# A transformer layer on one core: the MLP's down-projection by seven block products over pairs of weight blocks

## The chip, the core and the metric

The kernel runs on one core of a Trainium2 chip. The core has a matrix engine (TensorE, PE in the profile; its loads of the stationary operand are PEld), a vector engine (VectorE, DVE), a scalar engine (ScalarE, ACT), a general engine (GpSimd, POOL) and an engine that issues transfers (SyncE, SP). Each engine works through its own queue in order, and waits on semaphores for the others. Matrix products end in PSUM, eight banks of 128 x 512 float32, which TensorE, VectorE and ScalarE use here and GpSimd does not; everything else is in SBUF or in DRAM. The metric is the device time of one execution in microseconds. The kernel before took 2886.45 us (median of three runs, 2884.72 to 2888.83).

## What is computed

One layer of a hybrid model on 2048 tokens of width 1024: retention and attention, an output projection, a gated residual, and then an MLP whose activation is a squared ReLU. Only the MLP and the last norm are touched by the change:

```python
def _sqrelu_mlp(h, w1, w2):
    return jnp.square(jax.nn.relu(h @ w1)) @ w2

    h2 = _modulate(_rmsnorm(x, norm2_g), sh2, sc2)
    x = x + g2 * _sqrelu_mlp(h2, w_ff1, w_ff2)
...
    return _rmsnorm(x, final_norm_g)
```

`w_ff1` is 1024 x 4096 and `w_ff2` is 4096 x 1024, all in float32.

## The kernel before

The kernel is one program in three overlapping stages; the schedule is written out by hand (`tc.manual_schedule()`), so the order of the code is the order of each engine's queue. Until about 1575 us it does the projections, retention, attention and the output projection; functions are put into numbered steps by `on(k, phase, ...)`, and the last of these steps already holds the beginning of the MLP (`prelude`). From 1606 us on it does nothing but the MLP.

**Precision.** Every float32 operand of a product is split into a high and a low float16 part (`split16`, lines 70 to 72: ScalarE writes the high part, VectorE or GpSimd subtracts it and writes the low part). A product is then three matmuls: high by high, high by low, low by high.

**The up-projection** (`up_part`, lines 1705 to 1714) is done by seven block products in place of eight. The tokens are taken in two halves of 1024 (`halves`); the 4096 columns of `w_ff1` in 16 blocks of 256. For one half and one block the weights are four tiles `a11` to `a22` (halves of the 1024 rows by 128 columns). Sums of them (`s1` to `s4`, `sum_w1`, GpSimd, line 1641) and of the tokens (`h_pair`, made once for each half, stored in DRAM as `hf` and held in SBUF) enter seven products of 4 x 3 matmuls with 512 columns each. Each product has a PSUM bank to itself (`pu`, four banks), and `up_out` adds the seven to running sums in SBUF on VectorE, straight from PSUM (line 1735), once on ScalarE (line 1740). Then come the ReLU (ScalarE, line 1723), the square (GpSimd, `r * r`, line 1724) and the split (ScalarE and VectorE, lines 71 and 72).

**The down-projection** (`down`, lines 1766 to 1775) is an ordinary one. For a half and a block, each of the eight groups of 128 tokens and each of the two halves of the 1024 output columns takes 2 x 3 matmuls into a bank of PSUM (`pd`), and VectorE adds the bank to the accumulator of those tokens in SBUF (line 1775). The rows of `w_ff2` are fetched for each block in each half of the tokens, so twice (`ws`), scaled by the gate on GpSimd (line 1696) and split (lines 71 and 72).

**The order of the work.** The main loop at the end of `layer_kernel` goes over 32 blocks (16 for each half). In a block, all seven up products come first, then the sixteen down groups; small jobs of the other engines are put in between by hand: the sums and splits of the next block's `w_ff1` (`sum_w1`, `form_w1`, lines 1641, 1650 and 1651), the making of `w_ff2` (`make_w2`), the remaining sums of the second half's tokens (`h_pair(1, ...)`), the end of the first half (`ending`: squares, root, scaling, storing, loading the second half's accumulators). `rest` holds the last steps of the last tile of the attention stage (`transpose_x`, `modulate`, `shift_`, `store_h`), which the main loop works off in its first blocks.

## Time and profile before

| what | value |
|---|---|
| median of three runs | 2886.45 us (2884.72 to 2888.83) |
| the profiled execution | 2882.76 us, of which its span 2881.0 us |
| mean granted TensorE clock | 0.990 |
| TensorE busy with matmuls | 2732.5 us, 95% of the span |
| VectorE busy | 2119.7 us, 74% |
| GpSimd busy | 1524.2 us, 53% |
| ScalarE busy | 1430.4 us, 50% |
| matmuls of the up-projection | 3 lines x 896 = 2688 |
| matmuls of the down-projection | 3 lines x 1024 = 3072 |

How to read the lines shown later: a group of instructions is given as line, engine, operation, what it writes and reads, how often, then its busy time in us and the mean of one in ns, and after the second bar the idle time of its engine just ahead of it with what ended that. A matmul's own duration (some 380 ns) is longer than its distance from the next one, since matmuls follow each other in a pipeline; the distance is what counts, and it is read from the number of matmuls in a stretch of time. In a table of windows each engine has its busy time and, in brackets, the number of its instructions.

### The profile page before, as it was taken

Reading aid. Unit: us, or ns where it says so; the run is one execution under the profiler, and the core shown is the slowest. Engines: PE = TensorE matmul, PEld = TensorE weight load, DVE = VectorE, ACT = ScalarE, POOL = GpSimd, SP = SyncE. Lnnn points to the kernel's source line nnn. Section 1 sums busy time; section 2 is a strip of 40 time slices with the busy share of each in tenths; the row PEclk is TensorE's granted clock in tenths of the full one; section 3 lists DMA queues with packets and bytes.
Section 4 is the critical chain, followed back from the end, with each engine's and each line's share of the span. In section 5 each row is a group of like instructions: output and inputs, shape, how many; then the busy total and the mean of one; then the engine's idle time right before and its main releaser. Section 6 shows DMA issues by size and latency. Waiting matters only on the chain. (4 is left out here: it accounts for less than half of the span.)

```text
span 2881.0 us, 45242 instructions
## 1 busy us (share of the span) xinstructions
PE 2732.5 (95%) x17152; PEld 1455.9 (51%) x17152; DVE 2119.7 (74%) x3324; ACT 1430.4 (50%) x2419; POOL 1524.2 (53%) x1289
## 2 busy tenths in 40 slices
PE   7999999988899999999998899999999999999998
PEld 2545644545566666666565344444444444444443
DVE  4856777478878778777875577777777777777776
ACT  3634752237777777777776233342333333333332
POOL 2623762447667568776776465663443434444432
PEclk9999999999999999999999999999999999999999
DMA  7478667562112122332224623231114411111111
GB/s 258 130 254 300 207 203 230 169 196 63 55 62 78 59 69 86 93 98 63 89 80 165 223 81 97 82 97 59 59 59 155 152 59 59 59 48 48 52 44 59
DMA packets 249656, 323.87 MB, mean 112 GB/s; under 512 B 105111, under 2 KB 156311, under 8 KB 247646
## 3 DMA queue, kind: packets, MB, share of 16 engines
q1 hardware_dynamic: 249150, 319.93, 34.4%
q8 instruction: 135, 2.21, 0.3%
q10 hardware_dynamic: 288, 1.05, 0.1%
q14 instruction: 83, 0.68, 0.1%
HBM read 249.45 MB, written 71.46 MB: 111 GB/s over the span
## 5 line engine op out<-in xcount | busy, mean ns | idle before, releaser
L180 DVE TENSOR_REDUCE nm<-mp 128x1 f32<-128x512 f32 (+1 forms) x576 | 389.8, 684 | 155.3 <-PE mp L167 126.6
L221 POOL TENSOR_TENSOR plo<-p,phi 128x1024 f16<-128x1024 f32 x160 | 352.7, 2206 | 164.9 <-ACT phi L214 136.2
L210 ACT ACTIVATE p<-st 128x512 f32<-128x512 f32 x576 | 337.9, 598 | 181.0 <-PE st L205 107.3
L1772 PE MATMUL pd<-w2hi,uhi 128*128 128x512 f16 x1024 | 388.0, 379 | 12.6 <-DVE acc L1775 12.4
L1773 PE MATMUL pd<-w2lo,uhi 128*128 128x512 f16 x1024 | 388.0, 379 | 0.6 <-DVE w2lo L72 0.6
L1774 PE MATMUL pd<-w2hi,ulo 128*128 128x512 f16 x1024 | 388.1, 379 | 0.0
L1775 DVE SCALAR_TENSOR_TENSOR acc<-pd,sc,acc 128x512 f32<-128x512 f32 x512 | 366.0, 738 | 5.7 <-PE pd L1774 5.6
L1712 PE MATMUL pu<-hf,w1f 128*128 128x512 f16 x896 | 340.9, 380 | 2.4 <-DVE q L1735 2.0
L1713 PE MATMUL pu<-hf,w1f 128*128 128x512 f16 x896 | 340.9, 381 | 0.0
L1714 PE MATMUL pu<-hf,w1f 128*128 128x512 f16 x896 | 340.8, 380 | 0.0
L214 ACT ACTIVATE phi<-p 128x1024 f16<-128x1024 f32 x288 | 303.9, 1055 | 0.0
L646 PE MATMUL pso<-wlo,h 128*128 128x512 f16 (+1 forms) x816 | 295.8, 363 | 2.4 <-DVE wlo L543 2.4
L645 PE MATMUL pso<-whi,h 128*128 128x512 f16 (+1 forms) x816 | 296.2, 363 | 1.0 <-ACT whi L542 1.0
L647 PE MATMUL pso<-whi,h 128*128 128x512 f16 (+1 forms) x816 | 295.5, 362 | 0.0
L223 DVE TENSOR_TENSOR plo<-p,phi 128x512 f16<-128x512 f32 x256 | 245.7, 961 | 15.8 <-ACT phi L214 14.7
L237 PE MATMUL o<-wv,plo 128*128 128x65 f16 x2304 | 235.0, 193 | 19.3 <-POOL plo L221 9.9
L238 PE MATMUL o<-wv,phi 128*128 128x129 f16 x2304 | 242.7, 220 | 0.0
L237 PEld LDWEIGHTS <-plo 128*128 128x128 f16 x2304 | 205.8, 98 | 64.7 <-POOL plo L221 20.8
L204 PE MATMUL st<-qr,ks 128*128 128x512 f16 x576 | 220.3, 382 | 14.9 <-ACT p L210 13.3
L1724 POOL TENSOR_TENSOR r<-r 128x512 f32<-128x512 f32 x64 | 66.4, 1041 | 295.2 <-ACT r L1723 295.2
L205 PE MATMUL st<-qr,ks 128*128 128x512 f16 x576 | 220.7, 383 | 0.1
L167 PE MATMUL mp<-ks,qr 128*128 128x512 f16 x512 | 196.4, 384 | 21.5 <-DVE nm L180 21.1
(331 smaller groups left out, 5414.0 us busy)
## 6 DMA issues: line engine op xcount, KB each, us to landing
wm<-in_w_ff SPq DMA_DIRECT2D x64, 512.0 KB, 5.4
w1r<-in_w_ff SPq DMA_DIRECT2D x64, 512.0 KB, 4.0
ws<-in_w_ff SPq DMA_DIRECT2D x124, 256.0 KB, 3.2
wmr<-in_w_mod SPq DMA_DIRECT2D x32, 512.0 KB, 5.6
hf<-hp SPq DMA_DIRECT2D x56, 256.0 KB, 3.2
hf<-hf SPq DMA_DIRECT2D x14, 1024.0 KB, 4.9
wst<-in_w_in SPq DMA_DIRECT2D x20, 512.0 KB, 6.6
wm<-in_w_mod SPq DMA_DIRECT2D x32, 256.0 KB, 7.1
```

The costliest lines, as they stand in the source:

```text
L180: nc.vector.tensor_reduce(dst, src, axis=AX.X, op=ALU.max, negate=True)
L210: nc.scalar.activation(self.p[kt // 2][:, kt % 2], self.s.pop(kt), AF.Exp, scale=HD**-0.5)
L214: nc.scalar.activation(hi, self.p[j], AF.Copy)
L221: nc.gpsimd.tensor_tensor(lo, p, hi, op=ALU.subtract)
L237: mm(o[:, : HD + 1], lo[:, i, c], v[:, : HD + 1], start=False, stop=False)
L1712: mm(pu[i], whi, hi, start=k == 0, stop=False)
L1713: mm(pu[i], whi, lo, start=False, stop=False)
L1714: mm(pu[i], wlo, hi, start=False, stop=k == 3)
L1772: mm(ps, uh, wh, start=f == 0, stop=False)
L1773: mm(ps, uh, wl, start=False, stop=False)
L1774: mm(ps, ul, wh, start=False, stop=f == NF - 1)
L1775: nc.vector.scalar_tensor_tensor(acc[:, c], ps, sc2, acc[:, c], op0=ALU.mult, op1=ALU.add)
```

## The change

The down-projection is also done by seven block products. Two neighbouring weight blocks make a superblock (16 for the two halves together, 8 for each). In it the squared activations of a block are four tiles of 128 x 512 (`a11` to `a22`: halves of the 256 columns by halves of the 1024 tokens), and the rows of `w_ff2` four tiles `b11` to `b22` of 128 x 512. Seven products of four token groups, two blocks and three matmuls each take the place of eight. For this

- GpSimd makes four sums of the squared activations of each block (`sum_r`), and seven tiles rather than four are split (`split_r`); the square moves from GpSimd to ScalarE (`square_r`);
- the gated rows of `w_ff2` and their four sums are made once for each of the 16 blocks, while the first half is at work (`w2_job`), stored in DRAM (`w2f_d`), and loaded from there for each superblock in both halves (`load_w2`);
- products share PSUM banks: three of the up-projection's running sums stay in one bank (`A`), which ScalarE copies out after the first, third and fifth of the seven products, in the middle of the group, before the next product adds to it; two more products share bank `C`; the down-projection's banks are used likewise (`down`, `down_out`: 28 additions by VectorE for a superblock, where 32 were for two blocks);
- the order changes: an up product (12 matmuls) and two token groups of the superblock before (12 matmuls) alternate. Such a pair is called a unit here; there are 14 for a superblock and 224 in all. The first four are done in the prelude, and the first 14 consist of the up product alone, since no superblock is ahead of them; at the end 28 token groups follow without an up product. The small jobs hang on the numbers of the units (`at`); a `w2_job` is spread over seven units and a new one starts every five, from unit 4 to unit 98, with the four `h_pair` in four of these 19 places;
- the scaling of the gate by 8192 becomes 4096, with the inverse factor changed to match, and the memory for the descriptors of dynamic transfers is made smaller.

```diff
     def up_part(b, n, k):
+        c = UP[n][2]
+        first = n in (0, 1, 3)
+        if k == 0 and first:
+            pu[c] = ff["ps1"].tile([P, HALF], F32, name="pu", tag="pu")
...
+        mm(pu[c], whi, hi, start=first and k == 0, stop=False, **more)
+        mm(pu[c], whi, lo, start=False, stop=False, **more)
+        mm(pu[c], wlo, hi, start=False, stop=k == 3, **more)
...
+    UP = [("a11", 0, "A"), ("a12", 3, "B"), ("s2", 1, "A"), ("s1", 5, "C")]
+    UP += [("s3", 2, "A"), ("a22", 4, "A"), ("s4", 6, "C")]
...
+        def copy(name):
+            x[name] = new_r(name)
+            nc.scalar.activation(x[name], ps, AF.Copy)
+
         if n == 0:
+            copy("v")
+        elif n == 1:
+            x["a11"] = relu(add(x["v"], x["v"]))
+        elif n == 2:
+            copy("q")
+        elif n == 3:
+            x["c"] = ps
+        elif n == 4:
+            copy("w")
+            nc.vector.tensor_tensor(x["w"], x["c"], x["w"], op=ALU.add)
+            x["a22"] = relu(x["w"])
+        elif n == 5:
+            x["a12"] = relu(new_r("r"), ps)
+        elif n == 6:
+            x["a21"] = relu(add(x["q"], x["q"]))
...
+    def rows_of(b, g):
+        at(g + 2, square_r, b, "a11")
+        at(g + 3, split_r, b, "a11")
...
+        at(g + 7, square_r, b, "a21")
+        at(g + 7, sum_r, b, "s1", "a21", "a22", ALU.add)
+        at(g + 7, sum_r, b, "s3", "a11", "a21", ALU.subtract, "a21")
+        at(g + 8, sum_r, b, "s2", "s1", "a11", ALU.subtract, "a11")
+        at(g + 8, sum_r, b, "s4", "a12", "s2", ALU.subtract, "a12")
+        at(g + 8, split_r, b, "s1", first=True)
...
+    DOWN = [("a11", "b11", "A", "u"), ("a12", "b21", "A", (0, 0)), ("s2", "t2", "B", "u")]
+    DOWN += [("s1", "t1", "C", (4, 1)), ("s4", "b22", "C", (0, 1)), ("s3", "t3", "D", (4, 1)), ("a22", "t4", "D", (4, 0))]
...
+    def w2_job(b, load, do):
...
+        def gate(i):
+            nc.gpsimd.tensor_tensor(x[i], x[i], g2b[0], op=ALU.mult)
...
+        plan = [(2, "b11"), (2, "b21"), (3, "t2"), (3, "t1"), (4, "b22"), (4, "t3"), (5, "t4")]
+        for k, w in plan:
+            do(k, form, w)
+            load(k + 1, store, w)
+        do(2, difference, x, "t1", "b12", "b11")
+        do(2, difference, x, "t2", "b22", "t1")
+        do(3, difference, x, "t3", "b22", "b12", "b12")
+        do(4, difference, x, "t4", "b21", "t2", "t1")
...
+    def down(s, n, m):
...
+        for j in range(2):
+            uh, ul = (us[2 * s + j, ua][:, i, m * P : (m + 1) * P] for i in range(2))
+            wh, wl = (w2[s, n][:, j, i] for i in range(2))
...
+            mm(ps, uh, wh, start=first and j == 0, stop=False, **more)
+            mm(ps, uh, wl, start=False, stop=False, **more)
+            mm(ps, ul, wh, start=False, stop=j == 1, **more)
...
+        for g in range(4, NU * 2 * NS):
+            b, n = divmod(g, 7)
+            s, u = divmod(g, NU)
+            for k in range(4):
+                up_part(b, n, k)
+            up_out(b, n)
+            if s == 0:
+                now(g, True)
+                now(g, False)
...
+            ms = (0, 1) if u % 2 == 0 else (2, 3)
+            down(s - 1, u // 2, ms[0])
+            now(g, True)
+            down_out(s - 1, u // 2, ms[0])
+            down(s - 1, u // 2, ms[1])
+            now(g, False)
+            down_out(s - 1, u // 2, ms[1])
```

How this moves the queues is seen best from three places. The first is GpSimd's queue around the last scaling of a tile in the attention stage (`xr<-xr,cy_f`), which the main loop's first transposes need. Before:

```order
746 L1489 TENSOR_SCALAR xr<-xr,cy_f 128x1024
747 L1724 TENSOR_TENSOR r<-r 128x512
748 L1724 TENSOR_TENSOR w<-w 128x512
749 L1724 TENSOR_TENSOR q<-q 128x512
750 L1504 TENSOR_TENSOR u<-u,s_240 128x512 x2
```

The same place now, as far as the last sum of the first `w2_job` of the main loop:

```order
747 L1490 TENSOR_SCALAR xr<-xr,cy_f 128x1024
748 L1765 TENSOR_TENSOR w2r<-w2r,g2b 128x1024 x2
749 L1551 TENSOR_TENSOR hs<-w2r 128x512
750 L1551 TENSOR_TENSOR hs<-w2r,hs 128x512
751 L1713 TENSOR_TENSOR s_21174<-q,w 128x512
752 L1713 TENSOR_TENSOR q<-v,q 128x512
753 L1637 TENSOR_TENSOR w1s<-w1r 128x512
754 L1551 TENSOR_TENSOR w2r<-w2r 128x512
755 L1713 TENSOR_TENSOR v<-s_21174,v 128x512
756 L1713 TENSOR_TENSOR r<-r,v 128x512
757 L1637 TENSOR_TENSOR w1s<-w1s,w1r 128x512
758 L1551 TENSOR_TENSOR hs<-w2r,hs 128x512
```

The three squares are gone; in their place stand two gate products of 1024 columns (`L1765`), the sums of `w_ff2`'s rows (`L1551`) and of the activations (`L1713`), among the sums of `w_ff1` (`L1637`) that were there.

The second place is VectorE's queue in the middle of a block, in the part of the first half in which `w_ff2` is made. Before, with the split of an activation (`ulo`), of `w_ff1` (`w1f`) and of `w_ff2` (`w2lo`) among the additions to the accumulators:

```order
1781 L72 TENSOR_TENSOR ulo<-q,uhi 128x512
1782 L1775 SCALAR_TENSOR_TENSOR acc<-pd,sc_244,acc 128x512
1783 L1651 SCALAR_TENSOR_TENSOR w1f<-w1r,sc_242,w1f 128x512
1784 L1775 SCALAR_TENSOR_TENSOR acc<-pd,sc_244,acc 128x512 x2
1787 L72 TENSOR_TENSOR w2lo<-ws,w2hi 128x512
1788 L1775 SCALAR_TENSOR_TENSOR acc<-pd,sc_244,acc 128x512 x2
```

Now (`us` and `ua` are the split activations, `w2f` the split tiles of `w_ff2`):

```order
1871 L1678 TENSOR_TENSOR v<-pu,v 128x512
1872 L72 TENSOR_TENSOR us_22485<-s_22453,us_22485 128x512
1873 L1650 SCALAR_TENSOR_TENSOR w1f<-w1r,sc_298,w1f 128x512
1874 L1824 SCALAR_TENSOR_TENSOR acc<-pd,sc_300,acc 128x512
1875 L72 TENSOR_TENSOR w2f<-w2r,w2f 128x512 x2
1876 L1824 SCALAR_TENSOR_TENSOR acc<-pd,sc_300,acc 128x512
1877 L72 TENSOR_TENSOR us_22533<-v,us_22533 128x512
```

Between two additions from PSUM there are now up to two or three operations with both inputs in SBUF, where there was one.

The third place is ScalarE's queue around an up-projection's copies from PSUM. Before, there was one (`v<-pu`), between the splits of `w_ff1` and the ReLUs:

```order
1549 L1650 ACTIVATE w1f<-w1r,sc_242 128x512
1550 L1740 ACTIVATE v<-pu 128x512
1551 L1650 ACTIVATE w1f<-w1s,sc_242 128x512 x2
1552 L1723 ACTIVATE r<-r,scu 128x512 x2
1553 L71 ACTIVATE uhi<-r 128x512
```

Now the copy of the third sum (`w<-pu`), after which TensorE goes on in the same bank:

```order
1558 L71 ACTIVATE us_21584<-r 128x512
1559 L1649 ACTIVATE w1f<-w1s,sc_298 128x512
1560 L71 ACTIVATE ua_21597<-v 128x512
1561 L71 ACTIVATE w2f<-hs 128x512 x2
1562 L1687 ACTIVATE w<-pu 128x512
1563 L1682 ACTIVATE w<-w,scu 128x512
```

The two rows `w2f<-hs` ahead of it read sums that GpSimd makes, and so does `us<-r`.

490 lines of the change are left out of this document (257 added, 233 removed).

## Prediction

> **What bounds the kernel now.** I read the page's busy times first, then a table of windows over the MLP, then the waits of TensorE in it. The page:
>
> ```profile
> PE 2732.5 (95%) x17152; PEld 1455.9 (51%) x17152; DVE 2119.7 (74%) x3324; ACT 1430.4 (50%) x2419; POOL 1524.2 (53%) x1289
> L1773 PE MATMUL pd<-w2lo,uhi 128*128 128x512 f16 x1024 | 388.0, 379 | 0.6 <-DVE w2lo L72 0.6
> L1713 PE MATMUL pu<-hf,w1f 128*128 128x512 f16 x896 | 340.9, 381 | 0.0
> ```
>
> The stage that the change touches lasts from the first of these rows to the second (TensorE's timeline):
>
> ```profile
> 1606.41 0.38 PE L1712 MATMUL pu<-hf,w1f 128*128 128x512 f16 x1
> ...
> 2868.29 0.38 PE L1774 MATMUL pd<-w2hi,ulo 128*128 128x512 f16 x1
> ```
>
> The windows give the number of matmuls in brackets:
>
> ```profile
> 1606.00:1650.00 44.00, 34.36 (x150) 15.26 (x149) 30.60 (x41) 15.89 (x27) 21.20 (x18) 0.96 0.72 250
> 1650.00:2200.00 550.00, 547.61 (x2535) 247.80 (x2533) 413.79 (x535) 191.87 (x309) 283.69 (x212) 1.00 0.24 75
> 2200.00:2300.00 100.00, 92.89 (x419) 41.13 (x417) 74.81 (x93) 36.90 (x61) 41.41 (x35) 0.98 0.55 195
> 2300.00:2850.00 550.00, 549.83 (x2548) 249.11 (x2547) 406.30 (x538) 176.42 (x281) 217.11 (x165) 1.00 0.15 48
> 2400.00:2600.00 200.00, 200.00 (x929) 90.69 (x927) 147.02 (x194) 64.37 (x102) 79.07 (x60) 1.00 0.18 57
> ```
>
> In the 200 us where TensorE never pauses, 929 matmuls run: 0.2153 us each. At that distance the stage's matmuls (2688 + 3072 of the table, less the 48 that run before 1606 us, plus 8 transposes: 5720) take 1231.5 us of the 1262. So TensorE bounds it. By windows it loses 11.7 us up to 1650 (44 - 150 x 0.2153), 4.2 up to 2200, 9.8 at the turn from the first half of the tokens to the second, 1.4 up to 2850. Who makes it wait:
>
> ```profile
> PE pd L1772 <- DVE acc L1775: 12.4, 17, 1.9
> PE bank L1494 <- POOL xr L1489: 5.2, 1, 5.2
> PE pu L1712 <- DVE q L1735: 2.0, 1, 2.0
> ```
>
> **The matmuls removed.** A superblock took 2 blocks x 16 groups x 6 = 192 down matmuls and takes 7 x 4 x 2 x 3 = 168. Over 16 superblocks 384 go, of the same shape: 384 x 0.2153 = 82.7 us. The up-projection keeps its 2688. Everything below asks how much of the 82.7 comes back. (The Trainium skill, "TensorE: Matmul & The Clock Gate", section Back-to-back issue gap, gives about 131 ns for a matmul of 512 columns in a stream of loads and matmuls; by that the 384 would be worth 50 us. The windows measure 0.2153 us here, close to the page's other formula for a warm array, so the trace decides.)
>
> **The side engines while `w_ff2` is made.** A unit has 24 matmuls, 5.17 us. Prices of VectorE and GpSimd, from the groups and from the rows' minimum, median and maximum:
>
> ```profile
> L1775 DVE SCALAR_TENSOR_TENSOR acc<-pd,sc,acc 128x512 f32<-128x512 f32 x512 | 366.0, 738 | 5.7 <-PE pd L1774 5.6
> L1735 DVE TENSOR_TENSOR q<-pu,q 128x512 f32<-128x512 f32 x64 | 43.3, 676 | 0.6 <-PE pu L1714 0.6
> L1651 DVE SCALAR_TENSOR_TENSOR w1f<-w1s,sc,w1f x54: 732/743/753, 2314.2 to 2822.3; 128x512 f16<-128x512 f32 x54
> L1651 DVE SCALAR_TENSOR_TENSOR w1f<-w1r,sc,w1f x41: 739/1099/1678, 2306.1 to 2812.0; 128x512 f16<-128x512 f32 x41
> L72 DVE TENSOR_TENSOR ulo<-r,uhi x64: 693/1112/1115, 1611.6 to 2840.9; 128x512 f16<-128x512 f32 x64
> L1641 POOL TENSOR_TENSOR w1s<-w1r x64: 1261/1270/2257, 1566.9 to 2779.9; 128x512 f32<-128x512 f32 x64
> L72 POOL TENSOR_TENSOR hp<-hb,hp x32: 1150/1160/1654, 1073.0 to 1914.9; 128x512 f16<-128x512 f32 x32
> 2866.44 2.36 POOL L1794 TENSOR_TENSOR acc<-acc,fgb 128x1024 f32<-128x1024 f32 x1 [1.26 <-ACT acc L1793]
> ```
>
> VectorE, a unit: two additions 1.48, three sums from PSUM in seven units 0.29, one split of `w_ff1` 0.74, one of an activation 0.69, and seven of `w_ff2` in five units 0.97: 4.17 us undisturbed. GpSimd: eight sums in seven units 1.45, two gates and four differences in five units 0.94 + 1.02: 3.41 us. Both fit into 5.17, but they hinder each other, which these four rows show:
>
> ```profile
> 2410.07 1.04 POOL L1724 TENSOR_TENSOR r<-r 128x512 f32<-128x512 f32 x1 [1.55 <-ACT r L1723]
> 2410.54 1.11 DVE L72 TENSOR_TENSOR ulo<-r,uhi 128x512 f16<-128x512 f32 x1 [1.37 <-ACT uhi L71]
> ...
> 2417.10 6.33 POOL L1696 TENSOR_TENSOR ws<-ws,g2b 128x512 f32<-128x512 f32 x4
> ...
> 2417.61 2.06 DVE L1775 SCALAR_TENSOR_TENSOR acc<-pd,sc,acc 128x512 f32<-128x512 f32 x3
> ```
>
> A split with both inputs in SBUF that meets GpSimd takes 1.11 in place of 0.69; an addition from PSUM beside GpSimd does not change (0.69 each); GpSimd's four gates take 1.58 each where a like operation has 1.27. With 3.4 such splits a unit and GpSimd under 66 to 80% of them, VectorE gains 3.4 x 0.42 x 0.66 to 0.8 = 0.9 to 1.1 us and comes to 5.1 to 5.3: at TensorE's pace, not far over it. VectorE may lag: a bank that it reads is written again only two units later (some 9 us), and the 20 units with an `h_pair` give time back, since VectorE has only 3.2 us there (no `w_ff2`), GpSimd 1.45 + (4 x 1.27 + 7 x 1.16) / 5 = 4.1. Of the 75 units with a `w2_job`, 65 have down groups. I take 0.2 us for each, **12 us**, with 0 (the lag is absorbed) and 48 (the two never overlap, below) as ends. The 4.2 us lost up to 2200 belong to the old order: -4. After unit 100 VectorE has 3.2 us a unit undisturbed. ScalarE, busy for 64 us of the 200 in the window above, gains two copies, four squares and three splits a block and loses four splits of `w_ff2`: five operations in seven units, which TensorE's 5.17 us a unit hides. The changed constants and the smaller descriptor memory add no instruction and cost nothing.
>
> **The first ten units** have 12 matmuls each (25.8 us in all), and GpSimd's queue is longer, as the order shows. The old waits for transfers ahead of it:
>
> ```profile
> 1589.10 1.12 POOL L1489 TENSOR_SCALAR xr<-xr,cy_f 128x1024 f32<-128x1024 f32 x1 [7.38 <-DMA x<-xr]
> ...
> 1615.78 1.12 POOL L1489 TENSOR_SCALAR xr<-xr,cy_f 128x1024 f32<-128x1024 f32 x1 [6.42 <-DMA x<-xr]
> ```
>
> The scaling at 1589 now stands behind two gates (4.7 us) that need `w_ff2`'s rows from a busy transfer queue: 0 to 5 us later. From the second scaling to the last sum of that `w2_job` GpSimd has two gates and ten sums, 17.4 us undisturbed, some 20 hindered; ScalarE's split of that sum stands ahead of the copy of `w` in unit 11, so units 12 and 13 end near 1648, where matmuls alone would end near 1635. That loses 13 us against 11.7 now: **+2**, from -8 (the transfers, now fewer at that moment, let the second scaling run earlier) to +14 (GpSimd's whole list of 32 us, hindered, is waited for).
>
> **Copies in the middle of a group.** The before has one copy a block and one wait for it; now `v`, `q` and `w`, by this row 0.58 each:
>
> ```profile
> L1740 ACT ACTIVATE v<-pu 128x512 f32<-128x512 f32 x32 | 18.5, 578 | 14.6 <-PE pu L1714 12.3 <-DMA hf<-hf 2.2
> ```
>
> `v` and `q` have a whole unit until TensorE adds to the bank. `w` has only the 12 down matmuls, 2.58 us, and waits in ScalarE's queue behind splits that need GpSimd. Such a split was emitted a unit earlier, so GpSimd must be over a unit late before it matters. I take **+2**; ends 0 and +10 (a few of the blocks).
>
> **SyncE, turn and end.** 112 stores and 112 loads of `w2f` replace 124 fetches. A load is issued five units (25.9 us) ahead; like transfers land in 4 to 5 us:
>
> ```profile
> w1r<-in_w_ff SPq DMA_DIRECT2D x64, 512.0 KB, 4.0
> hf<-hf SPq DMA_DIRECT2D x14, 1024.0 KB, 4.9
> ```
>
> So a queue held up by a late store is covered four units deep; without the cover a load costs its 4 us. At the turn the seven tiles of the second half are fetched one a unit, seven units ahead, where one was fetched every 2.58 us: of the 9.8 us lost I expect 3 to stay, **-7** (-10 to +5, if the accumulators' exchange is late). The end after the last matmul (12.3 us to the span's 2881.0) has one tile to finish rather than three: **-2** (-4 to +3).
>
> **The sum**: -82.7 + 12 - 4 + 2 + 2 - 7 - 2 = -79.7, on the profiled execution's 2882.76 us: 2803.1. The median of the runs shown lies 3.7 above that execution, so I forecast **2807 us**. All ends together reach from -109 to -7.
>
> **Rivals.**
> *VectorE and GpSimd take turns.* If a two-input operation of VectorE and one of GpSimd never overlap, a `w2_job` unit lasts 3.4 splits (2.40) + 3.41 = 5.8, 0.65 over TensorE's, in 65 units 42 us, and an `h_pair` unit 0.3 over in 20: 48 instead of 12, **2843**. For it: both sides in the rows above slow down. Against it: the split of 1.11 us had 0.57 us under the square and needed 0.54 after it, less than its 0.69, so some work is done meanwhile. The Trainium skill, "SBUF — State Buffer", section Who interferes with whom, states this turn-taking as a rule: the one that comes second blocks fully until the first is done. The rows here come near it without reaching it.
> *ScalarE is late with the copy of `w` everywhere.* If its queue is held by GpSimd so that the copy ends 5.9 us after the product, TensorE waits 3.3 us in each of the 31 blocks that follow: 102 us, **2907**, slower than before. It decides from 2.8 us a block on. For it: the order has two rows that read GpSimd's sums right ahead of the copy. Against it: in the second half (16 blocks) there is no `w_ff2` work, and GpSimd is idle for two thirds.
> *Everything is covered.* VectorE's lag is absorbed, the start gains 8, the turn and the end lose nothing: 12 + 10 + 2 + 3 + 2 less, **2778**.
>
> **How the numbers follow.** Forecast 0.60 (2790 to 2828), taking turns 0.22 (up to 2860), all covered 0.10 (2775 to 2790), the late copies 0.05, and 0.03 for a mixture that gives all back and ends where it was. From 2782 to 2852 lie the first, most of the second (0.16) and half of the third: 0.81. A measurement of this kernel tells 0.2%, 5.8 us, from no change: faster 0.92, the same 0.03, slower 0.05.
>
> **What would show it.** In the profile after: 2688 matmuls in three down lines; windows in the second half with about 465 per 100 us; between unit 14 and 98 (some 440 us) 2 to 3% fewer, VectorE busy over 95% there and GpSimd some 80%; the longest waits of TensorE before 1650 us, for ScalarE's `w`. I am wrong if TensorE waits for ScalarE or VectorE in the second half, if the first half's windows hold under 430 matmuls per 100 us, or if the turn still costs 10 us.

## The result, and the profile after

The changed kernel takes 2908.98 us (median of four runs, 2905.11 to 2910.06), the kernel before beside it 2885.59 us: a ratio of 1.0081, with a 95% interval of 1.0062 to 1.0099. It is slower, by 23 us, where 79 us less were forecast. The profiled execution took 2909.34 us, its span 2907.6.

TensorE does the smaller number of matmuls, as the page of the changed kernel shows:

```profile
PE 2674.7 (92%) x16768; PEld 1423.5 (49%) x16768; DVE 2144.3 (74%) x3209; ACT 1569.5 (54%) x2711; POOL 1609.6 (55%) x1275
```

Where the 384 matmuls went to is seen when the windows are cut at the units (24 matmuls each from unit 14 on): units 4 to 13, 14 to 97 (those with a `w2_job`), 98 to 125, 126 to 139 (the turn), 140 to 222.

```profile
1621.29:1674.97 53.68, 34.23 (x130) 14.25 (x129) 44.96 (x37) 26.60 (x48) 38.21 (x24) 0.81 0.60 216
...
1674.97:2186.99 512.02, 454.01 (x2018) 200.17 (x2016) 418.83 (x456) 240.72 (x423) 351.11 (x217) 0.96 0.51 165
2186.99:2336.21 149.22, 145.84 (x674) 65.71 (x672) 115.42 (x139) 66.87 (x115) 65.97 (x45) 1.00 0.43 150
2336.21:2415.58 79.37, 74.11 (x338) 33.12 (x337) 53.76 (x64) 40.13 (x68) 32.35 (x21) 0.98 0.52 172
2415.58:2845.52 429.94, 429.94 (x1994) 194.91 (x1993) 288.87 (x365) 171.50 (x293) 132.02 (x92) 1.00 0.23 76
```

The last row is the second half: 1994 matmuls without a pause, 0.2156 us each and 5.18 us a unit (429.94 / 83). The second row is where the gain was lost: 84 units that TensorE could do in 435 us took 512, so 77 us are lost there. VectorE is busy for 418.83 us of them, 4.99 a unit and less than TensorE's 435, and yet it is what TensorE waits for most often (all of the MLP, us in total, times, longest):

```profile
PE pd L1809 <- DVE acc L1824: 47.3, 32, 4.3
PE pu L1666 <- ACT w L1687: 26.4, 6, 12.0
PE bank L1495 <- DVE al L1455: 13.0, 1, 13.0
PE pu L1666 <- DVE w L1699: 6.7, 1, 6.7
PE pu L1666 <- ACT v L1687: 6.2, 1, 6.2
PE pd L1809 <- DVE accu L1824: 4.2, 4, 1.9
```

The first row is the additions to the accumulators that come late, 32 times; the second the copy of `w` in the middle of a group, six times. In units 14 to 97 alone the two are 34.4 and 21.6 us. VectorE's own waits in units 14 to 97 say what it does in the 93 us in which it is not busy: it waits for the high parts that ScalarE writes.

```profile
DVE w1f L1650 <- ACT w1f L1649: 42.5, 28, 4.5
DVE us L72 <- ACT us L71: 40.3, 19, 6.2
DVE w2f L72 <- ACT w2f L71: 5.1, 5, 2.3
```

ScalarE in its turn waits there for VectorE's sums, ahead of the ReLUs (140.7 us for `w`, `v` and `q` together), and for 58.5 us for GpSimd; the largest row of each:

```profile
ACT w L1682 <- DVE w L1699: 63.4, 12, 8.6
...
ACT w2f L71 <- POOL w2r L1765: 42.5, 20, 3.8
```

So the engines wait for each other in a ring, and the rows alone do not tell which of them is the first cause; the experiments do.

One stall of 6.9 us in unit 18 from near, in a timeline of GpSimd (first row, two gate products) and VectorE:

```profile
1695.51 5.54 POOL L1765 TENSOR_TENSOR w2r<-w2r,g2b 128x1024 f32<-128x1024 f32 x2
...
1696.02 0.74 DVE L1824 SCALAR_TENSOR_TENSOR acc<-pd,sc,acc 128x512 f32<-128x512 f32 x1
1696.68 2.17 DVE L72 TENSOR_TENSOR us<-q,us 128x512 f16<-128x512 f32 x1
1699.00 2.60 DVE L72 TENSOR_TENSOR w2f<-w2r,w2f 128x512 f16<-128x512 f32 x1
1701.76 1.52 DVE L72 TENSOR_TENSOR w2f<-w2r,w2f 128x512 f16<-128x512 f32 x1
1703.20 0.74 DVE L1824 SCALAR_TENSOR_TENSOR acc<-pd,sc,acc 128x512 f32<-128x512 f32 x1
```

Three splits of 0.69 us take 6.3 us beside GpSimd, and the addition at 1703.20, the longest of TensorE's 32 waits (4.3 us), stands behind them. The addition at 1696.02, from PSUM, keeps its 0.74.

### The profile page after: what moved, and what is told of

Read it like the earlier page. It is cut to its first block, busy times and chain, and to the rows that moved or that the text cites. A ratio compares the mean times of both kernels' runs of the same rounds, so it can differ in the third digit from the quotient of the medians.

```text
span 2907.6 us, 44941 instructions
## 1 busy us (share of the span) xinstructions
PE 2674.7 (92%) x16768; PEld 1423.5 (49%) x16768; DVE 2144.3 (74%) x3209; ACT 1569.5 (54%) x2711; POOL 1609.6 (55%) x1275
## 4 chain that ended last, share of the span: by engine, by line
PE 61%; DVE 15%; POOL 6%; issue 6%; DMA 6%; ACT 5%; SPq 1%; POOLq 0%; DVEq 0%; ACTq 0%
PE pso L646 5%; PE pso L647 5%; PE pso L648 5%; PE pd L1809 4%; PE pd L1811 4%; PE pd L1810 4%; PE pu L1666 4%; PE pu L1668 4%; PE pu L1667 4%; PE o L239 3%; PE mp L168 3%; PE st L205 3%; PE st L206 3%; DVE w2f L72 2%; DVE plo L224 2%
## 5 line engine op out<-in xcount | busy, mean ns | idle before, releaser
L1666 PE MATMUL pu<-hf,w1f 128*128 128x512 f16 x896 | 346.2, 386 | 41.2 <-ACT w L1687 26.4
L1667 PE MATMUL pu<-hf,w1f 128*128 128x512 f16 x896 | 346.1, 386 | 0.0
L1668 PE MATMUL pu<-hf,w1f 128*128 128x512 f16 x896 | 345.5, 386 | 0.0
L1713 POOL TENSOR_TENSOR s<-q,w 128x512 f32<-128x512 f32 x32 | 43.3, 1355 | 453.4 <-ACT q L1708 453.4
L224 DVE TENSOR_TENSOR plo<-p,phi 128x512 f16<-128x512 f32 x256 | 243.4, 952 | 15.6 <-ACT phi L215 14.4
L1824 DVE SCALAR_TENSOR_TENSOR acc<-pd,sc,acc 128x512 f32<-128x512 f32 x320 | 234.9, 742 | 11.5 <-PE pd L1811 10.8
L1809 PE MATMUL pd<-w2t,us 128*128 128x512 f16 x512 | 196.0, 383 | 41.7 <-DVE acc L1824 39.7
L239 PEld LDWEIGHTS <-phi 128*128 128x128 f16 x2304 | 205.7, 97 | 21.4 <-issue 0.9
L1810 PE MATMUL pd<-w2t,us 128*128 128x512 f16 x512 | 196.3, 383 | 0.0
## 6 DMA issues: line engine op xcount, KB each, us to landing
w2t<-w2f SPq DMA_DIRECT2D x112, 512.0 KB, 4.2
wm<-in_w_ff SPq DMA_DIRECT2D x64, 512.0 KB, 5.3
w1r<-in_w_ff SPq DMA_DIRECT2D x64, 512.0 KB, 5.1
wmr<-in_w_mod SPq DMA_DIRECT2D x32, 512.0 KB, 5.1
w2r<-in_w_ff SPq DMA_DIRECT2D x32, 512.0 KB, 4.9
```

Of the source, the lines that this page charges most:

```text
L239: mm(o, hi[:, i, c], v[:, :VW], start=False, stop=last)
L1666: mm(pu[c], whi, hi, start=first and k == 0, stop=False, **more)
L1667: mm(pu[c], whi, lo, start=False, stop=False, **more)
L1668: mm(pu[c], wlo, hi, start=False, stop=k == 3, **more)
L1810: mm(ps, uh, wl, start=False, stop=False, **more)
```

## The experiments

Three theories were tried against each other. **A**: ScalarE's queue holds up the copies and splits, because it waits for GpSimd's gate products and sums. **B**: VectorE, with GpSimd stretching its operations, has too much to do. **C**: SyncE's queue is held by stores and fetches come late. The table has every kernel that ran: the median and the ratio to the kernel before on the same chip, and from the traces (us) the length of units 0 to 13, of units 14 to 97, and what VectorE and GpSimd were busy for in the latter. The kernels ran on different chips, and the medians of the kernel before beside them lie between 2880.3 and 2885.6 us; differences of a few us are therefore read from the ratios.

| kernel | median, ratio (95% interval) | units 0-13 | units 14-97 | VectorE | GpSimd |
|---|---|---|---|---|---|
| the changed kernel | 2909.0, 1.0081 (1.0062 to 1.0099) | 96.4 | 512.0 | 418.8 | 351.1 |
| e1_no_jobs | 2840.1, 0.9852 (0.9832 to 0.9872) | 88.2 | 452.5 | 298.2 | 196.1 |
| e3_later | 2918.6, 1.0124 (1.0107 to 1.0141) | 88.7 | 532.5 | 419.4 | 353.5 |
| e4_order | 2910.1, 1.0096 (1.0080 to 1.0113) | 96.2 | 517.9 | 428.8 | 358.0 |
| e5_no_stores | 2898.8, 1.0056 (1.0036 to 1.0076) | 96.8 | 506.2 | 419.0 | 350.8 |
| e6_unread | 2906.5, 1.0088 (1.0070 to 1.0105) | 89.9 | 521.7 | 421.3 | 367.5 |
| e7_no_low | 2851.2, 0.9892 (0.9876 to 0.9909) | 84.5 | 470.3 | 345.5 | 346.9 |
| e8_no_gpsimd | 2839.3, 0.9848 (0.9833 to 0.9862) | 76.5 | 467.2 | 359.6 | 202.3 |
| e9_start_pairs | 2897.1, 1.0048 (1.0033 to 1.0063) | 80.1 | 517.7 | 431.2 | 360.8 |
| e10_sums_vector | 2910.7, 1.0104 (1.0089 to 1.0119) | 88.6 | 524.5 | 428.1 | 274.2 |
| e11_all_vector | 2904.4, 1.0084 (1.0067 to 1.0101) | 85.5 | 517.1 | 423.4 | 208.4 |
| e12_together | 2872.9, 0.9971 (0.9960 to 0.9982) | 74.9 | 495.8 | 443.0 | 209.7 |
| e13_even | 2884.5, 1.0011 (1.0002 to 1.0021) | 84.4 | 508.7 | 424.8 | 354.5 |
| e14_even_together | 2865.0, 0.9949 (0.9934 to 0.9964) | 69.4 | 498.7 | 447.3 | 215.8 |
| e15_even_gpsimd | 2849.5, 0.9891 (0.9876 to 0.9906) | 67.3 | 488.9 | 425.5 | 340.9 |
| e16_lag | 2886.5, 1.0015 (1.0005 to 1.0024) | 92.4 | 499.0 | 427.7 | 353.4 |
| e17_lag_even | 2838.9, 0.9851 (0.9835 to 0.9868) | 65.5 | 470.4 | 441.5 | 350.4 |
| e18_loads | 2831.8, 0.9833 (0.9817 to 0.9850) | 66.4 | 469.8 | 437.2 | 346.9 |

**Without the jobs.**

```diff
-        nc.sync.dma_start(w, w2f_d[s % NS][n])
+        nc.sync.dma_start(w, w2f_d[0][n])
...
+            if isinstance(job, int) and job > 1:
+                continue
```

> Leaves out the making of w_ff2's tiles for blocks 2 to 15; every superblock loads the tiles of the first, so the loads stay and the output is not the reference's. The changed kernel spends 6.1 us on each of units 14 to 97, where its matmuls need 5.17. All three theories (A: ScalarE's queue order, B: VectorE and GpSimd saturated, C: SyncE's queue held by stores) expect the stalls of these units to go but for those of the four h_pair: A, B and C say 5.2 to 5.4 us a unit there, 45 to 75 us less than the changed kernel, so 2835 to 2865. If it stays above 2890, the jobs are not the cause and the copies from PSUM alone are.

The jobs of the blocks 2 to 15 are left out here, and the loads always take the first superblock's tiles. It ran in 2840.1 us. Units 14 to 97 lose 17 us in place of 77, all in units 60, 61, 74 and 75, where an `h_pair` is at work. So the jobs carry most of the loss, and the `h_pair` a part of their own.

**SyncE.**

```diff
-            nc.sync.dma_start(w2f_d[b // 2][W2.index(w)][:, b % 2], x.pop(("left", w)))
+            f = x.pop(("left", w))
+            if b < 2:
+                nc.sync.dma_start(w2f_d[b // 2][W2.index(w)][:, b % 2], f)
```

> Makes all of w_ff2's tiles but stores only those of the first superblock, which every superblock then loads; the output is not the reference's. C (SyncE waits in its queue for VectorE's splits ahead of each store, so fetches go out late, GpSimd's gates wait for them, and ScalarE and TensorE behind) expects 40 us or more less than the changed kernel, 2870 or below. A and B expect 0 to 15 us less, 2894 to 2909, since the splits stand where they stood.

SyncE's longest waits in the changed kernel are indeed for the splits that it is to store (from 1606 to 2200 us):

```profile
SPq L1775 <- DVE w2f L72: 297.2, 100, 12.6
```

But without the stores of the blocks 2 to 15 (the loads take the first superblock's tiles again) only 7 to 10 us come back (by the ratios and by the medians, from two executions), 6 of them in units 14 to 97. C is no more than a small part.

**ScalarE's queue, first two tries.** In the one, a job's gates come two units after its fetch and the splits a unit later; in the other ScalarE copies bank `C` after its first product, in place of the last copy of `A`, and the last two up products change places.

```diff
+        [(3, "b11"), (3, "b21"), (4, "t2"), (4, "t1"), (5, "b22"), (5, "t3"), (6, "t4")],
...
-            do(1, gate, i)
+            do(GATE_AT[bool(b)], gate, i)
```

> The same operations; each gate of a block but the first is issued two units after its fetch in place of one, and each split one unit later, so that ScalarE finds GpSimd's results ready. A (ScalarE's splits of w_ff2 wait for GpSimd in front of the copy of w) expects 30 to 60 us less than the changed kernel, 2850 to 2880. B expects within 10 us of 2909, since no work goes. C expects no gain or a loss, since the stores and the next fetch come later too: 2905 to 2925.

```diff
+    UP += [("s3", 2, "A"), ("s4", 6, "C"), ("a22", 4, "A")]
...
         elif n == 3:
-            x["c"] = ps
+            copy("w")
         elif n == 4:
-            copy("w")
-            nc.vector.tensor_tensor(x["w"], x["c"], x["w"], op=ALU.add)
-            x["a22"] = relu(x["w"])
+            x["a22"] = relu(add(x["w"], x["w"]))
...
-        at(g + 7, split_r, b, "a12")
+        at(g + 8, split_r, b, "a12")
```

> The same number of operations; the last two up products change places, and ScalarE copies C after its first product while VectorE adds it to A straight from PSUM, so that TensorE comes back to A a whole unit later (7.8 us of cover in place of 2.6). A expects most of TensorE's waits for the copy of w to go, 30 to 55 us less than the changed kernel: 2855 to 2880. B expects the lost time to return as waits for VectorE's additions from PSUM, within 12 us of 2909. C expects 10 to 30 us less.

The first is slower than the changed kernel by about 10 us (units 14 to 97 by 20), which B and C allowed and A did not; why it is slower was not followed up. The second is as slow as it, and the waits of TensorE (from 1660 to 2260 us) show why that decides little:

```profile
PE pd L1807 <- DVE acc L1822: 36.9, 24, 3.6
PE pd L1807 <- ACT ua L71: 9.4, 5, 4.9
PE pd L1809 <- DVE ua L72: 9.1, 5, 2.8
...
PE pu L1666 <- ACT w L1687: 4.0, 2, 2.8
```

The waits for the copy of `w` are nearly gone (4.0 us), but the edit brought the split of `a12` a unit later, and TensorE now waits 18.5 us for that. What stays untouched are the late additions of VectorE, 36.9 us (34.4 in the changed kernel).

**The waits alone, VectorE's part alone, GpSimd's part alone.** These three tell A and B apart. The first keeps the work and takes the waits for GpSimd's results away (each gate product is cut into two halves, and GpSimd is busy for 16 us more), the second takes VectorE's low parts away, the third GpSimd's products and sums.

```diff
-            nc.gpsimd.tensor_tensor(x[i], x[i], g2b[0], op=ALU.mult)
+            for c in range(2):
+                spare = xp.tile([P, HALF], F32, name="hs", tag="hu", bufs=3)
+                col = slice(c * HALF, (c + 1) * HALF)
+                nc.gpsimd.tensor_tensor(spare, x[i][:, col], g2b[0][:, col], op=ALU.mult)
...
-            split16(f[:, 0], f[:, 1], x[w])
+            split16(f[:, 0], f[:, 1], x[RAW.get(w, w)])
```

> GpSimd does its products and sums of w_ff2 as before, but into spare tiles that nobody reads; the splits of w_ff2 read the rows as fetched. So the work of every engine stays and only ScalarE's and VectorE's waits for GpSimd's results go (the result leaves out the gate and the sums of w_ff2). Theory A (the copy of w and the splits stand in ScalarE's queue behind splits that wait for GpSimd): 40 us or more of the 77 lost in units 14 to 97 come back and some 10 at the start, 2850 to 2870 us. Theory B (VectorE and GpSimd hinder each other so much that in four of a block's seven units their work does not fit into TensorE's time): the loss stays, 2890 to 2912 us.

```diff
-            split16(f[:, 0], f[:, 1], x[w])
+            nc.scalar.activation(f[:, 0], x[w], AF.Copy)
```

> VectorE's seven low parts of w_ff2 in each job are left out (the high part is stored and loaded twice), GpSimd's and ScalarE's work and ScalarE's waits for GpSimd stay. Theory A: at most 15 us come back, 2893 us or more. Theory B: taken in turn, GpSimd and VectorE's operations in SBUF need 20 us a block and 14.6 a job, of which 4.8 go; for 7 units that is 33.7 us in place of 40.5 against TensorE's 36.3, so the units with a job fit: 35 to 55 us come back, 2853 to 2873 us.

```diff
-            do(1, gate, i)
...
-        do(2, difference, x, "t1", "b12", "b11")
-        do(2, difference, x, "t2", "b22", "t1")
-        do(3, difference, x, "t3", "b22", "b12", "b12")
-        do(4, difference, x, "t4", "b21", "t2", "t1")
```

> GpSimd's two products and four sums of each job are left out (the splits read the rows as fetched; the result leaves out the gate and the sums of w_ff2), all of VectorE's and ScalarE's work stays. Both theories expect a gain here; A the one of the spare tiles again and no more (2850 to 2870), B more than from the low parts, since 9.8 us of 14.6 a job go: 50 us in units 14 to 97 and 10 at the start, 2840 to 2855 us. What is left is the h_pair at units 60 and 74, the turn and the end.

Units 14 to 97 in the windows of the first,

```profile
1665.76:2187.47 521.71, 457.24 (x2018) 200.90 (x2017) 421.29 (x462) 238.88 (x423) 367.47 (x246) 0.95 0.52 170
```

of the second,

```profile
1657.74:2128.06 470.32, 443.59 (x2017) 198.86 (x2016) 345.49 (x370) 246.47 (x430) 346.87 (x222) 0.98 0.51 162
```

and of the third:

```profile
1650.74:2117.93 467.19, 442.48 (x2018) 198.65 (x2017) 359.58 (x460) 241.15 (x425) 202.34 (x141) 0.97 0.59 191
```

Without the waits nothing comes back in these units (522 us against 512). Without the low parts VectorE has 86 instructions less and 73 us less to do, and 42 us come back. Without GpSimd's part VectorE has as many instructions as in the changed kernel (460 and 456) and is still busy for 59 us less, since they are stretched less, and 45 us come back. A split of `w2r` there, minimum, median and maximum in ns,

```profile
L72 DVE TENSOR_TENSOR w2f<-w2r,w2f x91: 676/683/1757, 1657.5 to 2114.9; 128x512 f16<-128x512 f32 x91
```

and in the changed kernel:

```profile
L72 DVE TENSOR_TENSOR w2f<-w2r,w2f x51: 674/1095/2604, 1683.1 to 2185.2; 128x512 f16<-128x512 f32 x51
```

A falls as the first cause in these units: what brings time back is less for VectorE to do, be it fewer instructions or less stretched ones. Neither brings all of it: 35 and 32 us are still lost.

**The start and the pairs.**

```diff
-        places = (6, 16, 20, 24, 27, 30, 31)
+        places = (6, 20, 28, 29, 30, 31, 31)
...
-            f = xp.tile([P, 2, 4, P], F16, name="hp", tag="hp", bufs=2)
+            tag = ("hp", "u")[hf * x["n"] % 2]
+            x["n"] += 1
+            f = xp.tile([P, 2, 4, P], F16, name="hp", tag=tag, bufs=2)
```

> Two small repairs at different places: the first job's products and splits are moved behind the last tiles' steps in the prelude, and an h_pair of the second half writes into four buffers in turn in place of two. If the start was lost to ScalarE's copy of a transposed tile behind the job's splits (13 us), the main loop starts at about 1608 in place of 1621 us, and some of it is lost again in the units 4 to 13; if the stalls at units 60 and 74 are ScalarE waiting for a buffer's store, 15 to 20 us come back there: together 2878 to 2890 us. If both are only VectorE and GpSimd in each other's way, at most 8 us come back: 2900 us or more.

In the changed kernel ScalarE stands 10 us at the first job's split, which waits for the gate product; the copy `ah` of a transposed tile, on which TensorE waits (13.0 us, the `bank` row above), is behind it:

```profile
1596.58 0.63 ACT L71 ACTIVATE w2f<-w2r 128x512 f16<-128x512 f32 x1 [9.99 <-POOL w2r L1765]
1598.88 0.63 ACT L71 ACTIVATE w2f<-w2r 128x512 f16<-128x512 f32 x1 [1.67 <-POOL w2r L1765]
...
1602.19 0.58 ACT L1453 ACTIVATE ah<-bank 128x512 f16<-128x512 f32 x1
```

With the job moved:

```profile
1587.25 0.58 ACT L1453 ACTIVATE ah<-bank 128x512 f16<-128x512 f32 x1
```

The copy comes 15 us earlier (13.5 if counted from the first up product), the first four units take 29.6 us in place of 42.7, and the wait of 13.0 us is gone. Units 60, 61, 74 and 75 lose 7 us in place of 24 (and the units 63 and 64 lose 9 that they did not lose). The stall there was ScalarE waiting for one of two buffers to be stored, with the copy of `w` behind it, as this piece of the changed kernel shows:

```profile
2043.76 0.63 ACT L71 ACTIVATE hp<-hb 128x512 f16<-128x512 f32 x1 [3.81 <-DMA hf<-hp]
...
2051.44 0.63 ACT L71 ACTIVATE hp<-hs 128x512 f16<-128x512 f32 x1 [4.45 <-DMA hf<-hp]
2051.98 0.58 ACT L1687 ACTIVATE w<-pu 128x512 f32<-128x512 f32 x1
```

The whole gain is only 10 to 12 us: what the start won in units 0 to 13 (16 us) is in part lost again in unit 15 (9 us), because the work of the first jobs is still to be done.

**Another engine for the sums.**

```diff
-        do(2, difference, x, "t1", "b12", "b11")
+        do(2, difference, x, "t1", "b12", "b11", None, nc.vector)
```

(and so for the three other sums; in the second kernel also `nc.vector` for the gate.)

> The four sums of a w2_job are made by VectorE in place of GpSimd; nothing is left out. Theory B, by which the two engines take turns on operands in SBUF: the price of a sum falls from GpSimd's 1.27 to VectorE's 0.69, so a job needs 12.3 us in place of 14.6 and seven units 37.2 in place of 40.4 (TensorE's 36.3): some 34 us come back, 2865 to 2885 us, although the busiest side engine gets more to do. Rival: VectorE alone is short of time (it is busy for 97 to 100% where TensorE waits); then 16 times 2.8 us more make it slower than the changed kernel, 2930 us or more.

> As the kernel before it in this call, and the two gate products of a w2_job are made by VectorE too. By turns a job needs 10.2 us and seven units 34.3, under TensorE's 36.3; but VectorE alone now has some 5.25 us a unit, at TensorE's 5.18, bursts aside. Theory B: about as fast as with the sums alone or up to 15 us faster, 2855 to 2885 us. Rival (VectorE alone is short): slower than the sums alone by 30 us or more.

Units 14 to 97 of the two:

```profile
1662.65:2187.11 524.46, 459.38 (x2018) 201.70 (x2017) 428.13 (x514) 243.76 (x427) 274.18 (x168) 0.95 0.52 170
```

```profile
1661.29:2178.37 517.08, 456.74 (x2017) 200.96 (x2016) 423.39 (x540) 243.03 (x426) 208.35 (x141) 0.95 0.52 171
```

GpSimd is relieved of 77 and 143 us, and nothing clear of the noise between chips comes back. So the form of B that counts both engines' time in one sum is wrong by its own numbers. VectorE has 58 and 84 instructions more and is busy for 9 and 5 us more, since the others are stretched less; its time stays, and so does the loss. The rival, that it gets slower by 2.8 us a job, falls too.

**Repairs together, and the sums of `w_ff1` later.** The first kernel joins the sums on VectorE, the four buffers and the later first job, gives the `h_pair`'s sums and low parts to VectorE too, and spreads the jobs over more units. The second is the changed kernel with one edit, the third and the fourth the repairs with that edit, and the fourth without any sum on VectorE.

```diff
-            g = 4 + 5 * i
+            g = 9 + 97 * i // 18
```

> The sums of the jobs by VectorE, those and the low parts of the second half's h_pair by VectorE too, four buffers for them, the first job behind the last tiles' steps, and the jobs of the main loop from unit 9 to 106 in place of 4 to 99 (w_ff2's loads two units later). If the repairs add up (34 for the sums, 12 measured for start and pairs, 10 for the pairs' work on VectorE, 10 for the spacing): 2840 to 2860 us, faster than both kernels.

```diff
-                        at(g + n, sum_w1, b + 1, *SUMS1[n])
+                        at(g + n + 3, sum_w1, b + 1, *SUMS1[n])
...
-                    at(max(g + n + 1, 4 + n // 2), form_w1, b + 1, n, first=True)
+                    at(g + n + 4 if b else 4 + n // 2, form_w1, b + 1, n, first=True)
```

> Nothing is left out or moved to another engine: the four sums and seven forms of the next block's w_ff1, with their fetch, come three units later, so that in each block GpSimd's sums of w_ff1 (now units 3 to 6) no longer fall into the units 0 and 1 with its sums of the activations. Every engine has the same work. Theory 'bursts' (VectorE has 5.0 of 5.18 us a unit and so cannot make up for the three or four units of a block in which GpSimd stretches its operations): 20 to 40 us of the 77 come back, 2868 to 2890 us. Theory 'total' (the loss goes by VectorE's occupied time alone, however it lies): the same as the changed kernel, 2900 to 2914 us.

> The four repairs of before together (jobs' sums and pairs on VectorE, four buffers, start, spacing: 2873 us) and the later sums of w_ff1. 'Bursts': another 15 to 30 us, 2843 to 2858 us. 'Total': 2868 us or more.

> As the kernel ahead of it, but the sums of the jobs and the pairs' work stay on GpSimd. By the two kernels with sums on VectorE, which changed nothing (2911 and 2904 us), the engine of the sums does not matter as long as VectorE's occupied time stays: within 8 us of the kernel ahead of it. If the gain of the four repairs came from the sums on VectorE: 15 us or more slower than that.

The time of e13_even, 2884.5 us, lies where theory "bursts" put it, but not for its reason, as its windows of units 4 to 13, 14 to 97 and of the turn show:

```profile
1616.92:1658.11 41.19, 29.74 (x129) 13.16 (x128) 32.34 (x31) 22.27 (x40) 25.83 (x17) 0.92 0.50 172
1658.11:2166.81 508.70, 451.12 (x2018) 199.37 (x2017) 424.78 (x459) 242.04 (x427) 354.47 (x222) 0.98 0.53 174
2316.70:2391.25 74.55, 72.82 (x338) 32.90 (x336) 53.47 (x62) 40.05 (x68) 32.72 (x22) 1.00 0.57 192
```

Of the 77 us only 3 come back; 12.5 come from units 4 to 13 and 4.8 from the turn. In units 14 to 97 the fifth unit of a block shrank from 9.3 to 7.2 us on average and five of the six others grew: for the most part the loss was only distributed otherwise. With the repairs, e14_even_together gains nothing there over e12_together (498.7 us against 495.8); its 6 to 8 us come from other places too. Both repaired kernels came out slower than the sum of the single gains said, 2873 and 2865 us. And putting the sums and the `h_pair`'s work back on GpSimd (e15_even_gpsimd) is worth 15.5 us, which neither of its expectations allowed: they had it the same or slower. VectorE is busy for 425.5 us there in place of 447.3.

**The low parts half a unit later.** What was left as the cause in units 14 to 97 was VectorE, by its occupied time or by its waits.

```diff
-        nc.vector.scalar_tensor_tensor(w[:, 1], src, sc1, w[:, 0], op0=ALU.mult, op1=ALU.subtract)
+        later(
+            lambda: nc.vector.scalar_tensor_tensor(w[:, 1], src, sc1, w[:, 0], op0=ALU.mult, op1=ALU.subtract)
+        )
...
     def now(g, first):
+        todo, lows[:] = list(lows), []
+        for fn in todo:
+            fn()
```

(`split_r` and the jobs' `form` likewise.)

> From unit 4 on, VectorE's low part of every split (activations, w_ff1, the jobs' w_ff2) stands half a unit behind ScalarE's high part in its queue, no longer right behind it; the work of each engine is the same. In the changed kernel VectorE is busy for 5.0 us of a unit's 6.1 and idle for 1.1, for the most part waiting for a high part. If that idle time is what is missing to TensorE's 5.18 (VectorE's work fits, but not with its waits), half or more of the 77 us come back: 2850 to 2875 us. If VectorE's occupied time and its bursts set the loss and the waits only fill what is left over: 2897 to 2915 us.

> The same on top of the best kernel so far (2849 us), where VectorE is busy for 5.07 us of 5.82. If the waits count: its loss of 54 us in units 14 to 97 halves, 2815 to 2832 us. If not: 2843 us or more.

On the changed kernel this brings some 20 us, less than "the waits" said and more than "the time" said; 13 of them in units 14 to 97. TensorE's waits there show what happened:

```profile
PE pu L1675 <- ACT w L1696: 37.9, 8, 11.7
PE pu L1675 <- ACT v L1696: 4.2, 1, 4.2
PE pu L1675 <- ACT q L1696: 3.3, 2, 2.0
PE pd L1825 <- DVE acc L1840: 1.8, 2, 1.6
```

VectorE's waits for high parts fall from 88 us to 51 in these units, but only 13 us come back: VectorE is busy for 9 us more, and the late additions (1.8 us now) give way to the copy of `w`, which is late behind splits of `h_pair` and of jobs in ScalarE's queue: theory A was the second in line. On the repaired kernel, where those splits wait less, units 14 to 97 lose 35 us in place of 54, which is less than the half that was expected. More than half of VectorE's idle time is gone there (63 to 29 us), but it is busy for 441.5 us in place of 425.5, more than TensorE's 435, so again only part of the waiting comes back. Of TensorE's waits in these units 15.6 us are now for loads.

**The loads' lead.**

```diff
-                at(max(NU * (s + 1) + 2 * n - 3, 12), load_w2, s, n)
+                at(max(NU * (s + 1) + 2 * n - 5, due(s, n)), load_w2, s, n)
```

> The best kernel so far (2839 us) with the loads of the split w_ff2 back at five units ahead of their use wherever the tile is stored by then (there they stand three units ahead). In its trace TensorE waits 21 us for such loads, which it never did in the changed kernel. If the lead of five units is the cover that the prediction took it for: 10 to 20 us come back, 2819 to 2830 us. If the loads are late because SyncE stands still at stores that wait for VectorE, the lead does not help where the tile is stored late: 2833 us or more.

It takes 2831.8 us, 5 to 7 less, between the two expectations. Its waits of TensorE over the MLP:

```profile
PE pd L1827 <- DVE acc L1842: 21.4, 18, 3.1
PE pu L1677 <- ACT w L1698: 18.2, 9, 4.7
PE pd L1827 <- DMA w2t<-w2f: 5.1, 1, 5.1
```

The waits for loads fall from 21 us to 5.1; part of them came back as waits for the copy of `w`. This is the fastest version: 1.7% faster than the kernel before (0.9833, 0.9817 to 0.9850) and faster than the changed kernel by more than 70 us, with the same 384 matmuls less.

## Why the prediction was wrong

The span grew by 26.6 us. By the terms of the prediction:

- **The matmuls removed**: -82.7 forecast, and they are gone: in the second half TensorE runs them at 0.2156 us each with no pause.
- **The side engines while `w_ff2` is made**: +12 - 4 forecast; 77 us are lost in units 14 to 97, so +77 - 4. This is the step that failed. VectorE's time in a unit with a `w2_job` was put at 5.1 to 5.3 us. A new job or `h_pair` starts every five units. In the 64 units from 14 to 97 whose turn is a job's, VectorE's time is 5.13 (328.1 us of 399.4), so its price was right; the mean of 4.99 is lower because in the 20 units whose turn is an `h_pair`'s it is 4.54. The failure is the next sentence, that VectorE "may lag" because a bank is written again only two units later, with 0.2 us a unit for it (65 times 0.2 is 13 and not 12, which decides nothing). VectorE had no waits in this sum. In 5.18 us, 5.13 leave 0.05 for them, and by the average VectorE is idle for 1.1 us a unit, nearly all of it in waits for ScalarE. 68 of the 77 us are lost in these 64 units, which last 6.24 us. That VectorE waits for ScalarE could have been read from the trace of before. There VectorE was idle for 136 us of the 550 up to 2200, and these are its waits in them:

```profile
DVE w1f L1651 <- ACT w1f L1650: 49.0, 31, 1.9
DVE ulo L72 <- ACT uhi L71: 39.6, 42, 2.0
DVE w2lo L72 <- ACT w2hi L71: 25.9, 18, 5.3
```

  These 114 us cost nothing as long as a quarter of its time was free. Where 99% of the unit is needed there is no room for them. Experiments e7 and e8 (less time) and e16 and e17 (fewer waits) both give time back, e6 (the waits for GpSimd alone) does not. How the 77 us divide between time and waits is not shown: when waits go, VectorE's operations are stretched more (e16: 37 us of waits less, 13 us of time back). The count of ScalarE's operations in the prediction holds for the second half; in the first the seven high parts of each job come on top. ScalarE is busy for 240.7 of the 512 us all the same, so its amount of work is not what cost the time.
- **The first ten units**: +2 forecast. From the first up product to unit 4 it takes 42.7 us where it took 30.9, and units 4 to 13 lose 25.7 us (53.7 less 130 x 0.2153) where 11.7 were lost: +26 in all. The +14 of the ten units is the upper end that was given, and the +12 of the four units ahead of them had no term. The step that failed looked at GpSimd's queue and the scaling in it alone; the job is put ahead of steps on ScalarE's queue too, and the wait of 13 us that this makes is the largest single one (e9).
- **Copies in the middle of a group**: +2 forecast, +10 the upper end. TensorE waits 26.4 us for `w`, six times, and 6.2 once for `v`. "A unit late before it matters" was right as a condition. In units 14 to 97 it was met four times: twice by the two buffers of an `h_pair`, which the prediction did not look at (16.6 us), and twice by jobs' splits that wait for GpSimd (5.0 us). These 21.6 us are part of the 77, the rest of the +26 above, and cannot be added: where the late additions go, these waits grow (e16), and the reverse (e4).
- **SyncE**: no cost forecast. 7 to 10 us by e5. TensorE never waits for a load in the changed kernel: the lead of five units covered the late stores, and with three it did not (e17 against e18).
- **The turn**: -7 forecast; 4.2 + 6.8 us are lost from unit 98 to 139 (149.2 and 79.4 us against 28 and 14 units of 5.18), 11 in all, as many as before from 2200 to 2850 us (9.8 + 1.4); nothing of the -7 came. e13 shows that 4.8 of them hang on when the sums of `w_ff1` are made; by what way was not followed.
- **The end**: -2 forecast, +6.5: the time after the last matmul, which the -2 was for, stayed within a microsecond. The 28 groups without an up product ahead of it had no term: they take 44.6 us for 169 matmuls (36.4), and TensorE waits 7.1 us for VectorE's additions. Before, 1.7 us were lost at that place. That there is no up product to hide the additions is a reading; no experiment was made on it.

Together -82.7 + 73 + 26 + 0 + 6.5, and 3 us by which the MLP begins later: 26, against 26.6 measured.

Of the rivals, *VectorE and GpSimd take turns* had the place right and the mechanism in part: the stretching is there. But its sum of the two engines' times is not what sets the pace, as e10 and e11 show, and its 48 us did not reach the 77. *ScalarE is late with the copy of `w` everywhere* had the sign right and, by luck, the time (2907 forecast for it, 2909 measured): TensorE waited for the copy in 6 blocks and not in 31, for 26 us and not for 102. Of the prediction's own signs of being wrong, the one on the first half's windows came true: units 14 to 97 hold 394 matmuls per 100 us where 430 were the limit.

What stays open: of the 35 us that e17 and e18 still lose in units 14 to 97, VectorE's 437 to 442 us against TensorE's 435 explain 2 to 7, and what the rest hangs on was not shown; nor why gates two units later (e3) cost 20 us there.

## What to carry to other kernels

An engine that works through its queue in order has as room what its period leaves after its work and after the waits that it already has for its neighbours; idle time that ends on a neighbour's result is not free time. It cost nothing here where the work took three quarters of the period, and stalled TensorE where the work took 99%. Where one engine's operation reads what another writes just ahead of it, half a unit between the two in the queues was worth some 20 us on the changed kernel, on which moving GpSimd's sums to VectorE was worth nothing. A job that is put into a start or a hand-over is to be followed on every queue that it touches, and the step looked for that the bottleneck needs next behind it.

## What the runs showed of the hardware

The stretching goes further than the rows of before showed (a split of an activation 0.69 to 1.11 us, one of `w_ff1` at most 1.68): a split with both inputs in SBUF took up to 2.60 us beside GpSimd's gate products. In the timeline of unit 18 the two splits from 1696.68 to 1701.60 and the gate products from 1695.51 on add up as if they had run one after the other: 2 x 2.36 + 2 x 0.69 = 6.1 us of undisturbed work in 6.1 us. So here the trace agrees with the rule of the Trainium skill that the prediction weighed ("SBUF — State Buffer", Who interferes with whom: the port pair that the two engines share is an exclusive lock, and a VectorE instruction with two SBUF inputs contends with GpSimd there; that the second blocks fully the page says of VectorE's two-port modes). The split of before that the prediction showed, 0.54 us after the square's end where 0.69 are needed, falls short of full blocking. And taking 143 us from GpSimd by giving VectorE 84 instructions more left VectorE's time within 5 us of what it was: for an engine that is hindered so, the work of its neighbour is a part of its own.

The granted clock is lower where TensorE pauses: 0.96 in units 14 to 97 and 0.81 in units 4 to 13, against 1.00 in the second half. The units between the stalls (14 to 17, 28 to 31) take 5.2 us each, so the clock is not what begins the loss. But it makes a stall dearer than its wait. In unit 18, after a wait of 4.3 us, the granted clock is 0.50 from 1705.0 to 1711.5 us, and matmuls stand up to 0.43 us apart in place of 0.22:

```profile
1703.99 0.38 PE L1809 MATMUL pd<-w2t,us 128*128 128x512 f16 x1 [4.26 <-DVE acc L1824]
...
1707.79 0.58 PE L1666 MATMUL pu<-hf,w1f 128*128 128x512 f16 x1 [1.92 <-ACT w L1687]
1708.17 0.63 PE L1667 MATMUL pu<-hf,w1f 128*128 128x512 f16 x1
```

Over units 14 to 97 TensorE is busy for 454.0 us with matmuls that take 435 at 0.2156: of the 77 us lost, 58 are pauses and 19 are matmuls at the lower clock behind them.
